# Where column weights are split, which engine squares the filters, and who ends the final norm, in a bidirectional encoder layer

## The chip, the cores and the metric

The kernel runs on one core of one Trainium2 chip, in one launch. The metric is the device time of that launch in microseconds (us); a median of several executions is compared with a median.

Five engines work side by side and wait for one another by semaphores: TensorE (PE in the rows; PEld is its loading of weights), VectorE (DVE), ScalarE (ACT), GpSimd (POOL), and SyncE (SP), whose queue issues all the DMAs spoken of here. TensorE's results land in PSUM; everything else on the chip lies in SBUF.

## The reference

One encoder layer on an input of 1024 positions by 1024 features, in float32:

```python
x = x + 0.5 * swiglu(rmsnorm(x), ffn1)      # D_FF = 2816
x = x + mixer(rmsnorm(x))
x = x + 0.5 * swiglu(rmsnorm(x), ffn2)
out = rmsnorm(x) * final_norm

# the mixer: one projection u = h @ w_in, whose columns go to three places
uc = centred_conv3(u[:, :1536])              # Hyena: x1, x2, v
k  = filters(positions)                      # small MLP, decay, scaled by rsqrt(sum k^2 + 1e-6)
z  = x1 * long_conv(v, k[0]);  z = x2 * long_conv(z, k[1])
y  = rwkv7(token_shift(u[:, 1536:3488]))     # two scans, forward and backward
g  = sigmoid(u[:, 3488:])                    # gates of the two branches
```

The filters are as long as the sequence on both sides, so the long convolutions are done as Fourier transforms.

## The kernel before

**Precision.** A float32 product of two matrices is made of three products of rounded halves: an operand x is split into hi (x rounded to the fast float32 format of TensorE) and lo (x - hi). `mm3` (L43 to L45) adds hi by hi, hi by lo and lo by hi. Activations are split once (`hThi`, `hTlo`); weights are split as they arrive: a DMA loads a block of 1024 rows by 128 columns as `w_st`, ScalarE casts it to `w_hi`, and VectorE or GpSimd subtracts to get `w_lo` (`split_from`, L30 to L37; `col_weights`, whose `lo_eng` picks the engine and is GpSimd unless said). There are two buffers of `w_st`, and three each of `w_hi` and `w_lo`.

**Stages.** ffn1 runs until about 770 us; the short convolution and the filters until 1020; the RWKV columns beside the long convolutions until about 1340; the RWKV scans and the gates until about 2070; ffn2 until 2790; its last group of down products with the final norm until the end. The order of instructions on each engine is set by the scheduler of the tile framework, which places them as their inputs come due; each engine then runs its own row in order.

**Short convolution and filters.** `mixer_in` makes twelve columns of `w_in` with `col_weights`. For each, `ShortConv` copies the product to `sh_u`/`sh_o` on ScalarE, adds two taps on VectorE (L550) and transposes on TensorE (`hy_tp`, L555). Between the columns it steps the generator `hyena_filters`, which makes four filters (two orders by two halves of 256 channels). A filter has eight steps `taps(r)`: a product `ps_h` (L420), a decay `ex` on ScalarE (L422), `kt` on VectorE (L424), its square `sq` on ScalarE (L432), and the square added to `acc` (L433); then `even_odd` (L438, L440) and products with the Fourier matrix (L448). After the last step the halves of `acc` are added (`ac2`, L499), and products with ones (L501, L506) give the sums by which the filter is scaled.

**RWKV columns beside the long convolutions.** `rwkv_columns` makes eighteen columns of `w_in`, each in two halves of 512 positions with 24 products of 128x512. `stage(j)` issues the load of column j's weights, `split(j)` makes its `w_hi` and `w_lo` on ScalarE and VectorE. Both are called in the middle of the column before:

```python
for k in range(KD):                       # KD = 8
    mm3(nc, ps, (w[0][:, k], w[1][:, k]), (hl[t][0][:, k], hl[t][1][:, k]), ...)
    if k == 3:
        if t == 0:
            split(j + 1)
            stage(j + 2)
        yield
```

At each `yield` the long convolution takes a step: forward products `hy_y<-hy_zz,F` (L627), ten or more VectorE operations `cxt` (L573, L618) that combine them and multiply by the filter's spectrum, inverse products `hy_y<-cxt,Dm` (L658), and the gate (L751, L755). A column's result goes through `rwkv_tile` (L1278: token shift on VectorE; L823 to L844: norm of the keys).

**The end.** In the last group of ffn2 eight columns d of `xT` are finished for each half t of the positions: nine products `pdn`, an add on VectorE (L226), then `nf.add`, which squares on ScalarE (`nm_sq`) and adds up on VectorE (`nm_acc`). `finish(t)` takes the reciprocal root `rms_r`, transposes `xT` back on TensorE into four PSUM buffers (L1782), multiplies each 128x512 block by `rms_r` and by the broadcast row `f_g` in one VectorE operation (L1785), and stores it (256 KB).

## Time and profile before

| | |
|---|---|
| median of 3 runs | 2841.01 us (2840.96 to 2841.77) |
| the profiled execution | 2847.4 us, of which 2845.6 us are the profiled span |
| TensorE busy | 2715.7 us, 95% of the span |
| VectorE busy | 1215.3 us, 43% |
| ScalarE busy | 893.4 us, 31% |
| GpSimd busy | 546.7 us, 19% |
| mean granted clock of TensorE | 0.973 of full speed |

The shares are means over stages that differ. Each row of a timeline gives the start, the length, the engine, the line of the kernel, the operation, the tile written and the tiles read, and in brackets how long the engine had been idle and what ended that.

### The profile page before, as it was taken

The numbers are of one execution on the slowest core, as the hardware profiler recorded it, in microseconds if no ns is written. First come the engines' busy times: TensorE is split into PE (matmuls) and PEld (weight loads), VectorE is DVE, ScalarE is ACT, GpSimd is POOL, SyncE is SP. The second block draws the span as 40 slices with busy tenths as digits, with TensorE's granted clock in tenths as the row PEclk, the third lists the DMA queues.
The fourth block names the chain that finished last, engine by engine and source line by source line (L and its number), as shares of the span: only waits on it lengthen the run. The fifth ranks groups of instructions, "written<-read, shape, count | busy, mean of one in ns | idle before, by whom it ended". The sixth has DMA issues, their size and how long they took to land. (4 is left out here: it accounts for less than half of the span.)

```text
span 2845.6 us, 45944 instructions
## 1 busy us (share of the span) xinstructions
PE 2715.7 (95%) x19440; PEld 2189.7 (77%) x19440; DVE 1215.3 (43%) x2132; ACT 893.4 (31%) x1507; POOL 546.7 (19%) x351
## 2 busy tenths in 40 slices
PE   8999999999988999999999998899999999999998
PEld 6888888888766777776787877776778888888787
DVE  4111010111547769897765767758631110101114
ACT  5111111111444542334554545532331111111113
POOL 2323232232422210000000000000033232332322
PEclk9999999999999999999999999898999999999999
DMA  5111111111341354554544325457521111111102
GB/s 127 56 41 53 44 52 45 49 48 44 112 150 63 105 169 149 173 154 129 173 133 134 104 87 183 144 178 249 151 77 56 48 48 41 56 41 49 49 26 93
DMA packets 402125, 276.43 MB, mean 97 GB/s; under 512 B 50643, under 2 KB 362527, under 8 KB 401280
## 3 DMA queue, kind: packets, MB, share of 16 engines
q1 hardware_dynamic: 401920, 273.50, 31.6%
q8 instruction: 153, 2.51, 0.4%
q14 instruction: 52, 0.43, 0.0%
HBM read 202.53 MB, written 70.91 MB: 96 GB/s over the span
## 5 line engine op out<-in xcount | busy, mean ns | idle before, releaser
L45 PE MATMUL pw<-hThi,w_lo 128*128 128x512 f32 (+1 forms) x1184 | 470.4, 398 | 15.5 <-DVE w_lo L1243 15.5
L43 PE MATMUL pw<-hThi,w_hi 128*128 128x512 f32 (+1 forms) x1184 | 472.2, 399 | 8.1 <-ACT sh_o L1265 4.5
L44 PE MATMUL pw<-hTlo,w_hi 128*128 128x512 f32 (+1 forms) x1184 | 470.8, 398 | 0.0
L33 ACT CAST w_hi<-w_st 128x1024 fp32r<-128x1024 f32 (+1 forms) x168 | 169.5, 1010 | 481.3 <-PE pw L44 185.2
L37 POOL TENSOR_TENSOR w_lo<-w_st,w_hi 128x1024 fp32r<-128x1024 f32 x100 | 239.9, 2399 | 401.0 <-ACT w_hi L33 394.7
L43 PE MATMUL pgu<-hThi,w_hi 128*128 128x512 f32 x704 | 279.1, 397 | 0.8 <-issue 0.8
L44 PE MATMUL pgu<-hTlo,w_hi 128*128 128x512 f32 x704 | 279.1, 396 | 0.3 <-POOL hTlo L37 0.2
L45 PE MATMUL pgu<-hThi,w_lo 128*128 128x512 f32 x704 | 278.9, 396 | 0.0
L43 PE MATMUL pdn<-g_hi,wd_hi 128*128 128x512 f32 x704 | 274.9, 390 | 1.8 <-DVE xT L226 1.7
L44 PE MATMUL pdn<-g_lo,wd_hi 128*128 128x512 f32 x704 | 274.6, 390 | 2.0 <-POOL g_lo L37 2.0
L45 PE MATMUL pdn<-g_hi,wd_lo 128*128 128x512 f32 x704 | 274.8, 390 | 1.7 <-POOL wd_lo L37 1.7
L45 PEld LDWEIGHTS pw<-hThi,w_lo 128*128 128x128 f32 (+1 forms) x1184 | 222.3, 188 | 69.3 <-DVE w_lo L1243 17.7
L43 PEld LDWEIGHTS pw<-hThi,w_hi 128*128 128x128 f32 (+1 forms) x1184 | 222.3, 188 | 63.0 <-ACT sh_o L1265 6.3
L226 DVE SCALAR_TENSOR_TENSOR xT<-pdn,xT 128x512 f32<-128x512 f32 x192 | 132.3, 690 | 314.8 <-PE pdn L45 314.8
L44 PEld LDWEIGHTS pw<-hTlo,w_hi 128*128 128x128 f32 (+1 forms) x1184 | 222.3, 188 | 54.2 <-issue 4.2
L209 DVE TENSOR_TENSOR silu<-silu,pgu 128x512 f32<-128x512 f32 x44 | 30.2, 687 | 449.5 <-PE pgu L45 449.5
L209 DVE TENSOR_TENSOR silu<-silu,pw 128x512 f32<-128x512 f32 x44 | 30.3, 688 | 445.8 <-PE pw L45 445.1
L37 POOL TENSOR_TENSOR wd_lo<-wdst,wd_hi 128x512 fp32r<-128x512 f32 (+1 forms) x112 | 132.1, 1180 | 333.3 <-ACT wd_hi L33 333.3
L37 POOL TENSOR_TENSOR g_lo<-silu,g_hi 128x512 fp32r<-128x512 f32 x88 | 113.5, 1289 | 399.0 <-ACT g_hi L33 399.0
L33 ACT CAST wd_hi<-wdst 128x512 fp32r<-128x512 f32 (+1 forms) x112 | 64.4, 576 | 379.2 <-PE pdn L44 365.7
L37 POOL TENSOR_TENSOR hTlo<-nm_h,hThi 128x512 fp32r<-128x512 f32 x16 | 23.6, 1477 | 737.2 <-ACT hThi L33 737.2
L43 PEld LDWEIGHTS pgu<-hThi,w_hi 128*128 128x128 f32 x704 | 132.4, 188 | 33.1 <-issue 1.2
(316 smaller groups left out, 4423.8 us busy)
## 6 DMA issues: line engine op xcount, KB each, us to landing
w_st<-in_ffn_w_gu SPq DMA_DIRECT2D x88, 512.0 KB, 3.7
w_st<-in_w_in SPq DMA_DIRECT2D x57, 512.0 KB, 3.8
wdst<-in_ffn_w_down SPq DMA_DIRECT2D x64, 256.0 KB, 2.8
wdst<-in_ffn_w_down SPq DMA_DIRECT2D x48, 192.0 KB, 2.5
d_kf<-kout SPq DMA_DIRECT2D x32, 256.0 KB, 2.3
hy_k<-d_kf SPq DMA_DIRECT2D x32, 256.0 KB, 3.1
w_st<-in_w_out SPq DMA_DIRECT2D x16, 512.0 KB, 4.4
d_X<-sh_x SPq DMA_DIRECT2D x12, 512.0 KB, 3.5
```

The source lines that it names most:

```text
L33: nc.scalar.copy(hi, src)
L37: eng.tensor_tensor(lo, src, hi.bitcast(F32), ALU.subtract)
L43: te.matmul(out, lhs[0], rhs[0], start=first, stop=False)
L44: te.matmul(out, lhs[0], rhs[1], start=False, stop=False)
L45: te.matmul(out, lhs[1], rhs[0], start=False, stop=last)
L209: nc.vector.tensor_tensor(sl, sl, pu, ALU.mult)
L226: nc.vector.scalar_tensor_tensor(xa, ps, 0.5, xa, ALU.mult, ALU.add)
```

## The change

Four places are edited.

- In the filters, the add of the squares (L433) goes from GpSimd to VectorE, and a `yield` is put between `ac2` and the product that uses it.
- In the short convolution, the twelve `w_lo` are subtracted on VectorE.
- In `rwkv_columns`, two columns are staged and split before the loop, and the loop splits column j + 2 and stages column j + 4, after the twelfth product of the first half. The 24 products of a half are put in another order: first the sixteen with `w_hi`, then the eight with `w_lo`. The numbers of buffers stay.
- In the final norm, `done` now scales `xT` in place by the weights of the norm on ScalarE, behind `nf.add`; the broadcast row `f_g` and its load go. `finish` multiplies by `rms_r` alone, the first block of each pair on VectorE, the second on ScalarE, into one tile of 128x1024, which is stored by one DMA of 512 KB.

```diff
@@ hyena_filters, taps
-                    nc.gpsimd.tensor_tensor(acc, acc, sq, ALU.add)
+                    nc.vector.tensor_tensor(acc, acc, sq, ALU.add)
@@ hyena_filters
             nc.vector.tensor_tensor(ac2, acc[:, 0], acc[:, 1], ALU.add)
+            yield
             ps = psh.tile([P, 512], F32, name="ps_h", tag="ps_h")
@@ rwkv_columns
-            stage(0)
-            stage(1)
-            split(0)
+            for j in range(2):
+                stage(j)
+            for j in range(2):
+                split(j)
+                stage(j + 2)
...
-                    for k in range(KD):
-                        mm3(nc, ps, (w[0][:, k], w[1][:, k]), (hl[t][0][:, k], hl[t][1][:, k]), k == 0, k == KD - 1, te)
-                        if k == 3:
+                    products = [(0, x, k) for k in range(KD) for x in range(2)] + [(1, 0, k) for k in range(KD)]
+                    for i, (a, b, k) in enumerate(products):
+                        te.matmul(ps, w[a][:, k], hl[t][b][:, k], start=i == 0, stop=i == 3 * KD - 1)
+                        if i == 11:
                             if t == 0:
-                                split(j + 1)
-                                stage(j + 2)
+                                split(j + 2)
+                                stage(j + 4)
                             yield
@@ mixer_in
-            weights = lambda t: col_weights(nc, wp, I["w_in"][:, ts(t, P)], KD)
+            weights = lambda t: col_weights(nc, wp, I["w_in"][:, ts(t, P)], KD, lo_eng="dve")
@@ the end
-            grow = c3.enter_context(tc.tile_pool(name="fg", bufs=1)).tile([P, D], F32, name="f_g")
-            nc.sync.dma_start(grow, bcast_row(I["final_norm"]))
+            fo = c3.enter_context(tc.tile_pool(name="fo", bufs=2))
+            def done(d, t):
+                x = xT[:, d, ts(t, 512)]
+                nf.add(x, t)
+                nc.scalar.activation(x, x, AF.Copy, scale=nf.g[:, d : d + 1])
...
+                    o = fo.tile([P, D], F32, name="f_o") if q % 2 else wp.tile([P, D], F32, name="f_w", tag="w_st")
                     for j in range(KD // 4):
...
-                        nc.vector.scalar_tensor_tensor(o, ps.rearrange("p a b -> p (a b)"), r[:, q : q + 1],
-                                                       grow[:, ts(j, 512)], ALU.mult, ALU.mult)
-                        nc.sync.dma_start(out[0, ts(ORDER[i], P), ts(j, 512)], o)
+                        flat = ps.rearrange("p a b -> p (a b)")
+                        if j:
+                            nc.scalar.activation(o[:, ts(j, 512)], flat, AF.Copy, scale=r[:, q : q + 1])
+                        else:
+                            nc.vector.tensor_scalar(o[:, ts(j, 512)], flat, r[:, q : q + 1], None, ALU.mult)
+                    nc.sync.dma_start(out[0, ts(ORDER[i], P), :], o)
```

Three places show how the scheduler's rows of instructions move. The first is VectorE's row in the first long convolution, just before its first inverse products; `cxt` are the convolution's operands, and the numbers behind the names count tiles. Before, this `w_lo` stands there:

```order
L573 TENSOR_TENSOR cxt_7327<-cxt_7263,cxt_7285 128x1024
L573 TENSOR_TENSOR cxt_7328<-cxt_7263,cxt_7285 128x1024
L1243 TENSOR_TENSOR w_lo_7351<-w_st_7258,w_hi_7350 128x1024
L573 TENSOR_TENSOR cxt_7370<-cxt_7325 128x512 x2
L573 TENSOR_TENSOR cxt_7373<-cxt_7327 128x512 x2
L573 TENSOR_TENSOR cxt_7376<-cxt_7370,cxt_7373 128x512 x2
```

And in the changed kernel:

```order
L574 TENSOR_TENSOR cxt_7335<-cxt_7271,cxt_7293 128x1024
L574 TENSOR_TENSOR cxt_7336<-cxt_7271,cxt_7293 128x1024
L1244 TENSOR_TENSOR w_lo_7359<-w_st_7167,w_hi_7358 128x1024
L574 TENSOR_TENSOR cxt_7378<-cxt_7333 128x512 x2
L574 TENSOR_TENSOR cxt_7381<-cxt_7335 128x512 x2
L574 TENSOR_TENSOR cxt_7384<-cxt_7378,cxt_7381 128x512 x2
```

VectorE's row is the same at this place; the `w_lo` in it is another. TensorE's row at the same place, around the first inverse products, is before:

```order
L45 MATMUL pw_7379<-hThi1_119,w_lo_7255 128x512
L43 MATMUL pw_7448<-hThi0_111,w_hi_7350 128x512
L44 MATMUL pw_7448<-hTlo0_112,w_hi_7350 128x512
L43 MATMUL pw_7594<-hThi1_119,w_hi_7350 128x512
L44 MATMUL pw_7594<-hTlo1_120,w_hi_7350 128x512
L43 MATMUL pw_7648<-hThi0_111,w_hi_7461 128x512
L44 MATMUL pw_7648<-hTlo0_112,w_hi_7461 128x512
L45 MATMUL pw_7448<-hThi0_111,w_lo_7351 128x512
```

And in the changed kernel, where `w_lo_7359` of VectorE's row is read only behind the inverse products:

```order
L1262 MATMUL pw_7602<-hThi1_119,w_lo_7263 128x512 x8
L1262 MATMUL pw_7656<-hThi0_111,w_hi_7358 128x512
L1262 MATMUL pw_7656<-hTlo0_112,w_hi_7358 128x512
...
L1262 MATMUL pw_7656<-hThi0_111,w_hi_7358 128x512
L659 MATMUL hy_y_7400<-cxt_7384,Dm_6967 128x256 x4
L659 MATMUL hy_y_7438<-cxt_7405,Dm_6967 128x256 x4
```

Before, TensorE reads the `w_lo` of VectorE's row six products after the last column ended; after, it comes to the inverse products first and reads that `w_lo` behind them. The third place is ScalarE's row at the end, for columns 4 and 5 of the last group; `nm_sq_23266` is column 4's square and `wd_hi_23272` is column 5's weight (in the row of before, `nm_sq_23264` and `wd_hi_23269`). Before:

```order
L33 CAST wd_hi_23249<-wdst_23247 128x384
L33 CAST wd_hi_23269<-wdst_23267 128x384
L92 ACTIVATE nm_sq_23224<-xT_18189 128x512
L92 ACTIVATE nm_sq_23244<-xT_18189 128x512
L33 CAST wd_hi_23289<-wdst_23287 128x384
L92 ACTIVATE nm_sq_23264<-xT_18189 128x512
```

And in the changed kernel:

```order
L1783 ACTIVATE xT_18189<-xT_18189,k_final_norm_76 128x512
L92 ACTIVATE nm_sq_23266<-xT_18189 128x512
L33 CAST wd_hi_23272<-wdst_23270 128x384
L1783 ACTIVATE xT_18189<-xT_18189,k_final_norm_76 128x512
L33 CAST wd_hi_23293<-wdst_23291 128x384
L33 CAST wd_hi_23314<-wdst_23312 128x384
```

Column 5's cast moved from ahead of column 2's square to behind column 4's, and a scale `xT` (L1783) follows each square.

## Rows read from the trace of the kernel before

**Rows 1.** Page: busy time, share of the span and instructions of each engine.

```profile
PE 2715.7 (95%) x19440; PEld 2189.7 (77%) x19440; DVE 1215.3 (43%) x2132; ACT 893.4 (31%) x1507; POOL 546.7 (19%) x351
```

**Rows 2.** Stretches: length, busy of PE PEld DVE ACT POOL, TensorE clock, DMA share, GB/s.

```profile
770.00:1020.00 250.00, 229.35 (x938) 166.99 (x937) 163.48 (x318) 120.27 (x191) 66.87 (x42) 0.97 0.30 99
2790.00:2846.00 56.00, 46.62 (x233) 38.26 (x231) 34.15 (x59) 19.62 (x34) 15.44 (x15) 0.92 0.35 118
1060.00:1332.00 272.00, 251.13 (x1150) 201.00 (x1149) 252.72 (x373) 94.97 (x136) 0.00 (x0) 0.97 0.50 151
1100.00:1110.00 10.00, 6.39 (x16) 4.62 (x16) 10.00 (x15) 1.04 (x1) 0.00 (x0) 0.66 0.37 112
```

**Rows 3.** Waits of TensorE, 1020 to 1400 us: total us, times, longest.

```profile
PE pw L45 <- DVE w_lo L1243: 15.5, 5, 6.5
```

**Rows 4.** Timeline near 1100 us, TensorE, then VectorE: start, length, [idle before].

```profile
1103.57 0.80 PE L45 MATMUL pw<-hThi,w_lo 128*128 128x512 f32 x1 [3.48 <-DVE w_lo L1243]
1097.02 5.36 DVE L573 TENSOR_TENSOR cxt<-cxt 128x512 f32<-128x512 f32 x7
```

**Rows 5.** Waits of VectorE, 1062 to 1332 us.

```profile
DVE hr_v L823 <- PE psA L820: 7.8, 3, 5.0
```

**Rows 6.** Timeline near 1175 us, TensorE, then VectorE.

```profile
1178.99 0.50 PE L45 MATMUL pw<-hThi,w_lo 128*128 128x512 f32 x1 [2.26 <-DVE w_lo L1243]
1173.01 0.17 DVE L823 TENSOR_SCALAR hr_v<-psA 128x16 f32<-128x16 f32 x1 [4.95 <-PE psA L820]
```

**Rows 7.** Groups by form, 770 to 1020 us: busy, mean ns of one, idle before.

```profile
L550 DVE SCALAR_TENSOR_TENSOR sh_o<-sh_u,k_cw,sh_o 128x1024 f32<-128x1024 f32 x20 | 31.6, 1582 | 21.7 <-ACT sh_o L545 21.6
L433 POOL TENSOR_TENSOR acc<-acc,sq 128x512 f32<-128x512 f32 x28 | 38.3, 1366 | 89.3 <-ACT sq L432 78.6 <-PE ps_k L448 10.7
L37 POOL TENSOR_TENSOR w_lo<-w_st,w_hi 128x1024 fp32r<-128x1024 f32 x9 | 21.9, 2433 | 73.5 <-ACT w_hi L33 67.4 <-PE ps_k L448 6.1
```

**Rows 8.** The same, 1020 to 1350 us, where GpSimd is idle.

```profile
L1243 DVE TENSOR_TENSOR w_lo<-w_st,w_hi 128x1024 fp32r<-128x1024 f32 x16 | 19.5, 1216 | 3.9 <-ACT w_hi L1242 3.9
L550 DVE SCALAR_TENSOR_TENSOR sh_o<-sh_u,k_cw,sh_o 128x1024 f32<-128x1024 f32 x4 | 5.1, 1278 | 0.0
```

**Rows 9.** Timeline in the first filter, VectorE, then GpSimd.

```profile
852.00 0.69 DVE L424 TENSOR_TENSOR kt<-ps_h,ex 128x512 f32<-128x512 f32 x1 [0.49 <-ACT ex L422]
871.95 1.26 POOL L433 TENSOR_TENSOR acc<-acc,sq 128x512 f32<-128x512 f32 x1 [3.94 <-ACT sq L432]
```

**Rows 10.** Waits of TensorE, 740 to 1020 us.

```profile
PE ps_h L501 <- DVE ac L499: 6.9, 4, 4.3
```

**Rows 11.** Timeline of VectorE, first two columns of the short convolution.

```profile
801.19 3.67 DVE L550 SCALAR_TENSOR_TENSOR sh_o<-sh_u,k_cw,sh_o 128x1024 f32<-128x1024 f32 x2 [10.62 <-ACT sh_o L545]
808.73 4.58 DVE L550 SCALAR_TENSOR_TENSOR sh_o<-sh_u,k_cw,sh_o 128x1024 f32<-128x1024 f32 x2 [3.74 <-ACT sh_o L545]
```

**Rows 12.** Timeline of the end: ScalarE, GpSimd, TensorE, VectorE.

```profile
2822.33 0.51 ACT L33 CAST wd_hi<-wdst 128x384 fp32r<-128x384 f32 x1 [1.61 <-DMA wdst<-in_ffn_w_down]
2826.88 0.63 ACT L92 ACTIVATE nm_sq<-xT 128x512 f32<-128x512 f32 x1 [0.46 <-DVE xT L226]
2826.50 1.02 POOL L37 TENSOR_TENSOR wd_lo<-wdst,wd_hi 128x384 fp32r<-128x384 f32 x1 [2.58 <-ACT wd_hi L33]
2823.77 0.47 PE L43 MATMUL pdn<-g_hi,wd_hi 128*128 128x512 f32 x1 [1.11 <-DVE xT L226]
2825.89 0.39 PE L43 MATMUL pdn<-g_hi,wd_hi 128*128 128x512 f32 x1
2837.82 3.65 PE L1782 MATMUL f_ps<-ident,xT 128*128 128x128 f32 x16 [2.33 <-issue]
2839.85 2.80 DVE L1785 SCALAR_TENSOR_TENSOR f_o<-f_ps,rms_r,f_g 128x512 f32<-128x512 f32 x4 [0.16 <-PE f_ps L1782]
```

**Rows 13.** DMA issues: queue, count, KB each, us to landing.

```profile
out<-f_o SPq DMA_DIRECT2D x16, 256.0 KB, 2.3
d_X<-sh_x SPq DMA_DIRECT2D x12, 512.0 KB, 3.5
```

More of the change, by code (lines that the diff above doesn't have):

```diff
@@ L1782, in finish @@
                             nc.tensor.transpose(ps[:, c, :], xT[:, 4 * j + c, ts(i, P)], ident)
-                        o = np_.tile([P, 512], F32, name="f_o", tag="nm_h") if j else \
-                            wp.tile([P, 512], F32, name="f_o", tag="w_st")
-                        nc.vector.scalar_tensor_tensor(o, ps.rearrange("p a b -> p (a b)"), r[:, q : q + 1],
-                                                       grow[:, ts(j, 512)], ALU.mult, ALU.mult)
-                        nc.sync.dma_start(out[0, ts(ORDER[i], P), ts(j, 512)], o)
+                        flat = ps.rearrange("p a b -> p (a b)")
[4 more added lines that the diff above has]
+                    nc.sync.dma_start(out[0, ts(ORDER[i], P), :], o)
             def pools():
@@ L1793, in hybrid_layer_kernel @@
             for _ in ffn(nc, pools, wp, xT, live["hl"], I["ffn2_w_gu"], I["ffn2_w_down"],
-                         lambda d, t: nf.add(xT[:, d, ts(t, 512)], t), finish):
+                         done, finish):
                 pass
```

## The prediction

> **What bounds the kernel now.** The page comes first: TensorE is busy 95% of the span [rows 1], so a change that adds no product and removes none can only win back pauses, and all pauses together are 130 us. The order of instructions differs in two stretches (the mixer's front, about 770 to 1380 us, and the last group of ffn2), so the rest is priced at nothing: the same rows on every engine, except the short stretch of ffn1's end, where three subtractions move to a VectorE that waits. The windows then show two different stretches. In the convolutions and columns, 1060 to 1332 us, TensorE is busy 251.1 of 272 us and VectorE 252.7: they wait for each other. In the short convolution, 770 to 1020, VectorE has 86 us idle, and TensorE loses 21. In the last 56 us TensorE loses 9 [rows 2].
>
> The waits of TensorE name the cause in the columns: five waits of 15.5 us in all for a `w_lo`, the longest 6.5 [rows 3]. The timeline shows what such a wait is. The `w_lo` is a subtraction of 1.22 us, but seven operations of the long convolution, 5.36 us from 1097.02 on, stand ahead of it on VectorE, and TensorE stands 3.48 us until it is done [rows 4, 8]. The clock follows: in the ten microseconds behind this wait the granted clock is 0.66, a mean between full speed (2.4 GHz) and half, and TensorE's busy time is 6.39 of 10 [rows 2]. So the reader should see a late operand on an engine that is itself full, not an engine that was asked too late.
>
> **The columns.** Splitting two columns ahead leaves VectorE's work as it is: eighteen subtractions, sixteen of them in this stretch at 1216 ns [rows 8]; two now stand ahead of the loop. What moves is who waits for which operation. In the order of the changed kernel the `w_lo` that stands in the first convolution's chain is read behind the inverse products, so the five waits of 15.5 us should go. But VectorE's operations before those inverse products are the same, and TensorE, which no longer stands at the `w_lo`, comes to them earlier and waits there for `cxt`. What can be won is therefore VectorE's idle time, since TensorE can only run ahead as far as VectorE does: 272 - 252.7 = 19.3 us [rows 2], the upper end. Not all of it comes from late `w_lo`. VectorE waits 7.8 us in three places for `psA`, the norm of the keys [rows 5]; the longest, 4.95 us, ends at 1173.01, and TensorE then stands 2.26 us for the `w_lo` that VectorE could not yet do [rows 6]. There each engine waits in turn for the other, and a weight two columns ahead cuts the circle. The rest of the idle time is waits for a Fourier product or an inverse product just issued, which the change leaves. I take the 4.95 us, as **5 us**. The lower end is 0: every wait for `w_lo` becomes one for `cxt`. A loss needs more VectorE work ahead of a chain, at most the two early subtractions, 2.4 us.
>
> With four stagings ahead and still two buffers of `w_st`, the load for column j + 4 waits until column j + 2 is split, and the next cast on ScalarE waits for that load; what is queued behind such a cast is the copy of a finished column out of PSUM, for which TensorE waits in turn. With the split two columns early the load has a whole column more to land; I put this at 0, and it lies within the 5.
>
> **The short convolution and the filters.** Twelve subtractions go from GpSimd (2433 ns each) to VectorE (1216 ns), and 28 adds of the squares from GpSimd (1366 ns) to VectorE [rows 7, 8]. No VectorE add of this form has a row in this place; a 128x512 operation with two inputs takes 0.69 us [rows 9], so VectorE gets 12 x 1.22 + 28 x 0.69 = 34 us more. Three effects reach TensorE.
> First, GpSimd's own work slows VectorE: the two taps (L550) take 1582 ns in the mean here and 1278 ns where GpSimd is idle [rows 7, 8]. The first two pairs, for which TensorE's transposes wait, take 3.67 and 4.58 us [rows 11]; undisturbed they are 2 x 1.28 = 2.56. In the changed order the first subtraction stands ahead of the first pair, inside VectorE's idle 10.62 us, and the second within the second pair, where it adds 1.22. That saves 3.67 - 2.56 = 1.1 and 4.58 - 2.56 - 1.22 = 0.8, together **1.9 us**. The upper end is the excess of all 20, 20 x 0.304 = 6.1.
> Second, at the end of each of the four filters TensorE stands for the sum of squares, 6.9 us in all, 4.3 of it in the first [rows 10]. The last add takes 1.26 us on GpSimd [rows 9] and 0.69 on VectorE: 0.57 sooner, four times, **2.3 us**. The ends are 0 and 6.9.
> Third, the cost. In the first filter no dense product lies beside the taps. VectorE waits there 0.49 us a tap for the decay factor [rows 9]; an add of 0.69 fills this and puts 0.20 more on each of seven taps, **1.4 us**. In the other three filters the 21 adds lie beside columns of the projection, under VectorE's idle 86 us, and I price them at nothing; if that cover were gone they would cost 21 x 0.69 = 14.5 us. The extra `yield` only puts other products ahead of the sum's, and costs nothing.
> Sum here: 1.9 + 2.3 - 1.4 = 2.8 us won, between 13 won (6.1 + 6.9) and 15.9 lost (1.4 + 14.5).
>
> **The end.** The two final operations of each pair now run on two engines. Now the last eight take until 2839.85 + 2.80 = 2842.65, while the transposes, 16 in 3.65 us behind 2837.82, end at 2841.47 [rows 12]. They run at 0.228 us each, and cannot start before a PSUM buffer is free, so the changed kernel ends its last block at 2841.47 + 0.68 = 2842.15: **0.5 us** won, not half of the VectorE time. Then the last store is 512 KB and not 256: stores of 256 KB land in 2.3 us, and the nearest transfer of 512 KB, also a write, in 3.5 [rows 13]: **1.2 us** lost. The Trainium skill (DMA: Bandwidth & Descriptors, Rules for kernel authors) speaks for the larger store: it asks for transfers of 1 MiB or more. By the fit that the skill gives (SBUF — State Buffer, The DMA setup-cost knee; 2 us and the bytes by 436 GB/s) 256 KB more cost an estimated 0.6 us, and the sum would be 0.6 us smaller. No row shows a large store at the end of the span, when nothing hides it.
> The half before wins: TensorE's wait of 1.11 us for VectorE between the transposes of the first half [rows 12] should go, since four of its eight operations are ScalarE's: **1.1 us** won.
> The new scales stand on ScalarE, and with them the casts of the down weights move. Column 5's cast ran at 2822.33, four columns of products ahead of its use; in the changed order it stands behind column 4's square, which starts at 2826.88 and takes 0.63 [rows 12]. So it ends at 2826.88 + 0.63 + 0.51 = 2828.02, and column 5's products, which start at 2825.89, nine products or 2.12 us behind column 4's first, start 2.1 us later. The low half follows on GpSimd, 1.02 us, while two products of 0.24 run: 0.5 more. Four transposes, at full clock half of the 0.228, fill 0.4 of it. So **2.2 us** lost; columns 6 and 7 have their casts in time, and the scales themselves lie under products. The ends are 0 (the scheduler's row waits less than I think) and, if TensorE's clock falls to 1.2 GHz behind this pause for the 27 products left, 2.2 + 27 x 0.24 = 8.7.
> Sum here: -0.5 + 1.2 - 1.1 + 2.2 = 1.8 us lost.
>
> **Sum.** -5.0 - 2.8 + 1.8 = -6.0 us. Against the profiled execution's 2847.4 us this is 2841.4; that execution lies 6.4 us above the median of the runs, so on the median 2841.0 - 6.0 = **2835.0 us**. A measurement of this kernel tells a change from none beyond about 0.2%, 5.7 us, so the forecast lies on this line, with 2835.3 its border.
>
> **Rivals.**
> *VectorE's idle time is all won.* The waits for `w_lo` go, none for `cxt` comes, and the clock stays up. For it: 15.5 us of waits with one name. Against it: VectorE is busy 93% of the stretch, and 10.00 of 10 us around the wait at 1103 [rows 2]. 19.3 + 2.8 - 1.8 = 20.3 us won, 2820.7 us.
> *The wait only changes its name.* VectorE sets the pace throughout, and what was waited at `w_lo` is waited at the inverse products. For it: VectorE's row is the same at the place shown in the order. Against it: the 4.95 us in which VectorE itself waits. 0 - 2.8 + 1.8 = 1.0 won, 2840.0 us, within 0.2%.
> *The filters' adds are exposed.* `kt`, the even and odd parts and the spectrum's sums form a chain through VectorE; an add put between them delays the next `kt` in the later filters too. 14.5 - 6.0 = 8.5 us lost, 2849.5 us. It is slower beyond 0.2% once 17 of the 21 adds are on the path (11.7 / 0.69). For it: the change's order puts each add ahead of the next `kt`. Against it: 86 us idle, and columns beside it.
>
> **How the numbers follow.** The forecast gets 0.45, its own range 2828 to 2841, three fifths of it below 2835.3; the first rival 0.13, the second 0.26 (nearly all within 0.2%), the third 0.16. So faster: 0.13 + 0.27 + 0.03 = 0.43; slower 0.17; within 0.2% the remaining 0.40. The range cuts about half of the outer rivals away on each side: 2822 to 2848.
>
> **What would show it.** Right: no wait for `w_lo` in the columns, new waits of the inverse products for `cxt`, VectorE's idle time from 1060 to 1332 about 5 us less; `psA` waited for less. L550 near 1280 ns; the wait for the sum of squares near 4.6 us; no idle time of VectorE ahead of `kt` in the first filter. At the end, a pause of about 2 us ahead of column 5's products, a last store of over 3 us. Wrong: TensorE's waits in the columns below 5 us in all (first rival) or above 20 (second); waits for `kt` or `eo` in filters 2 to 4 (third); a lower granted clock in a stretch where this text has no pause.

## The result and the profile after

The changed kernel takes 2824.69 us (median of 6 runs, 2821.21 to 2833.47); the kernel before takes 2842.59 beside it (6 runs, 2840.96 to 2846.41). The ratio is 0.9942, its 95% interval 0.9927 to 0.9956: 0.58% faster, some 16.5 us (12.5 to 20.8). The direction and the range held; the forecast was 10.3 us too high.

The profiled execution of the changed kernel took 2829.45 us, with a span of 2827.7 and a mean granted clock of 0.977: 17.9 us of span less than before. Its page has this row of busy times, which answers to [rows 1]:

```profile
PE 2707.4 (96%) x19440; PEld 2185.7 (77%) x19440; DVE 1229.4 (43%) x2164; ACT 909.0 (32%) x1531; POOL 480.3 (17%) x311
```

TensorE's busy time fell by 8.3 us at the same 19440 products (fewer of them ran at the slower clock), so about half of the gain is a pause less and half a product that ran faster. To see where the time went, the same product is looked up in both timelines of TensorE, and the differences of the starts are taken:

| start of | before | after | difference | products of TensorE ahead of it, before and after | gained in the stage, for the same products |
|---|---|---|---|---|---|
| the first transpose of the short convolution, `hy_tp` | 805.1 | 803.0 | -2.1 | 3445, 3445 | 2.1 |
| the last `ps_k` of the filters | 1021.1 | 1010.6 | -10.5 | 4258, 4271 | 11.3 |
| the last inverse product of the long convolutions | 1330.4 | 1317.2 | -13.2 | 5569, 5595 | 5.7 |
| the first product of the scans, `psA<-rl_x,rw_w` | 1343.3 | 1324.8 | -18.5 | 5612, 5612 | -0.6 |
| the last product of the gates, `mo_ps` | 2083.2 | 2062.5 | -20.7 | 16175, 16175 | 2.2 |
| the first transpose of the final norm, `f_ps` | 2808.1 | 2788.7 | -19.4 | 19288, 19288 | -1.3 |
| the last transpose | 2841.0 | 2823.1 | -17.9 | 19439, 19439 | -1.4 |

Two of these places don't stand at the same amount of work. TensorE's row was put in another order, so that 13 more of the 128x512 products of the projection stand ahead of the last `ps_k`, and 26 more ahead of the last inverse product; at the scans the count is equal again. Such products start 0.227 us apart at full clock, so these are 3.0 and 5.9 us, and the last column counts them in; this is an estimate. The starts alone would give 8.4, 2.7 and 5.3 us for the filters, the columns and the handover to the scans, and the last two of these would mislead. The busy times agree with the column. Here are the stretches from the first transpose to the last `ps_k` and from there to the scans (columns as in [rows 2]), before, then in the changed kernel:

```profile
805.00:1021.00 216.00, 200.10 (x813) 144.28 (x814) 144.49 (x281) 108.99 (x171) 57.72 (x36) 0.97 0.29 91
1021.00:1343.00 322.00, 297.16 (x1356) 237.91 (x1354) 278.13 (x418) 111.84 (x162) 0.96 (x1) 0.98 0.52 162
```

```profile
803.00:1011.00 208.00, 200.08 (x828) 147.20 (x829) 161.19 (x318) 111.11 (x173) 0.00 (x0) 0.98 0.31 97
1011.00:1325.00 314.00, 294.34 (x1342) 236.07 (x1343) 275.52 (x417) 110.83 (x159) 0.96 (x1) 0.98 0.54 167
```

TensorE's idle time fell from 15.9 to 7.9 us in the first and from 24.8 to 19.7 in the second.

What a single trace can tell is seen in kernels that share an order of instructions. With the final norm's edit alone, a kernel is the one before up to ffn2, and its starts in the table lie 0.3 to 1.1 us from those of before as far as the scans, and 3.8 at their last state product; with the columns' edit alone the filters are those of before, and end 2.3 us later. The seven traces that have the whole filters' edit and no dead work lie within 3.6 us of one another at the last `ps_k`. So up to 1340 us a difference of two or three us between two starts is not safe by itself, and the 2.2 us of the scans and gates are no gain of the change.

**The filters.** The waits of TensorE from 740 to 1020 us, of the changed kernel (total us, times, longest):

```profile
PE ps_h L502 <- DVE ac L499: 3.4, 1, 3.4
PE ps_h L420 <- DVE kt L424: 2.3, 3, 0.8
...
PE hy_tp L556 <- DVE sh_o L551: 0.7, 1, 0.7
```

And three of VectorE's groups by form, 760 to 1010 us:

```profile
L551 DVE SCALAR_TENSOR_TENSOR sh_o<-sh_u,k_cw,sh_o 128x1024 f32<-128x1024 f32 x20 | 25.6, 1279 | 8.1 <-ACT sh_o L546 8.0
L433 DVE TENSOR_TENSOR acc<-acc,sq 128x512 f32<-128x512 f32 x28 | 19.3, 689 | 3.7 <-ACT sq L432 3.7
L525 DVE TENSOR_TENSOR kout<-cxt 128x256 f32<-128x256 f32 x18 | 7.6, 422 | 1.9 <-DMA d_kf<-kout 1.8
```

The taps take 1279 ns, as forecast (1582 in [rows 7]); the sums wait once and not four times [rows 10]; VectorE does its 28 adds and the twelve subtractions without TensorE's waiting for it elsewhere. The windows show the rest (columns as in [rows 2]; the first answers to its first row):

```profile
770.00:1020.00 250.00, 238.30 (x990) 177.33 (x989) 185.01 (x365) 125.50 (x196) 6.54 (x5) 0.97 0.32 103
1050.00:1318.00 268.00, 250.95 (x1152) 201.29 (x1151) 251.84 (x378) 93.86 (x135) 0.96 (x1) 0.98 0.51 156
```

TensorE is busy 238.3 of 250 us and not 229.4, with 52 more products done in the window; VectorE's idle time fell from 86 us to 65.

**The columns.** The waits of TensorE from 1010 to 1400 us no longer hold a `w_lo` above 1 us (before: [rows 3]):

```profile
PE pw L1262 <- ACT sh_o L1270: 7.4, 2, 5.6
PE hy_y L659 <- DVE cxt L619: 2.4, 1, 2.4
PE pw L1262 <- ACT sh_o L1274: 2.2, 1, 2.2
```

And `psA` is waited for less (VectorE's waits, 1050 to 1320 us; before: [rows 5]):

```profile
DVE hr_v L824 <- PE psA L821: 4.4, 3, 2.7
```

So 15.5 us of waits with one name went; those whose releaser is ScalarE's copy of a finished column, 4.5 us before (longest 3.2), are 9.6; and of TensorE's idle time from the filters' end to the scans 5.2 us were won. The longest wait now is followed in the timelines of TensorE, ScalarE and VectorE, in this order:

```profile
1152.87 0.79 PE L1262 MATMUL pw<-hThi,w_hi 128*128 128x512 f32 x1 [5.58 <-ACT sh_o L1270]
```

```profile
1151.18 1.04 ACT L1317 COPY sh_v<-rw_kh 128x1024 f32<-128x1024 f32 x1 [3.26 <-issue]
1152.13 1.26 ACT L1270 ACTIVATE sh_o<-pw,k_mu 128x512 f32<-128x512 f32 x2
```

```profile
1149.70 1.40 DVE L1297 SCALAR_TENSOR_TENSOR rw_kh<-sh_o,k_kk,psA 128x512 f32<-128x512 f32 x2
```

TensorE needs the PSUM buffer that ScalarE empties at 1152.13. ScalarE stands 3.26 us ahead of that, because the reversed copy `sh_v` is next in its row and reads `rw_kh`, which VectorE starts at 1149.70, in line behind the convolution's `cxt`, and ends at 1151.10. In this place the column waits for VectorE as before, by way of another engine.

**The handover to the scans.** Here are SP's queue and TensorE before, then both in the changed kernel:

```profile
1339.09 0.42 SPq L899 DMA_DIRECT2D rl_x<-d_tw  x1
1343.29 1.16 PE L55 MATMUL psA<-rl_x,rw_w 64*128 64x128 f32 x16 [3.15 <-DMA rl_x<-d_tw]
```

```profile
1311.20 0.88 SPq L900 DMA_DIRECT2D rl_x<-d_tw  x1
1318.47 0.63 PE L762 MATMUL hy_t<-ident,hy_z 128*128 128x128 f32 x4 [0.87 <-DVE hy_z L756]
1320.26 0.50 PE L55 MATMUL pw<-hThi,w_hi 128*128 128x512 f32 x1 [1.16 <-ACT hy_zT L764]
1324.80 1.16 PE L55 MATMUL psA<-rl_x,rw_w 64*128 64x128 f32 x16
```

Before, `rl_x` was loaded behind the last inverse product, and TensorE stood 3.15 us for it. In the changed kernel the RWKV columns end first, the load goes 6 us ahead of that product, and this wait is gone. But nothing is won here: the 26 products of these columns that ran between the last inverse product and the scans now run earlier, TensorE waits 0.87 and 1.16 us in their place, and the granted clock from 1317 to 1325 us is 0.78, where it was 1.00 from the last inverse product to the scans before.

**The start of ffn2.** The -1.3 us of the table is no scatter. The stage takes 724.3 to 725.0 us in the twelve traces without the norm's edit and 726.2 and 726.3 in the two with it. The broadcast row `f_g` was loaded at its start; without that load the first two down weights are issued together, and GpSimd has two `wd_lo` in one go beside the reciprocal root of ffn2's norm. GpSimd and VectorE before, then GpSimd, VectorE and TensorE in the changed kernel:

```profile
2090.02 1.27 POOL L37 TENSOR_TENSOR wd_lo<-wdst,wd_hi 128x512 fp32r<-128x512 f32 x1 [3.15 <-ACT wd_hi L33]
2089.60 0.17 DVE L71 TENSOR_SCALAR rms_e<-rms_e 128x4 f32<-128x4 f32 x1
```

```profile
2068.85 2.50 POOL L37 TENSOR_TENSOR wd_lo<-wdst,wd_hi 128x512 fp32r<-128x512 f32 x2 [2.68 <-ACT wd_hi L33]
2068.90 1.25 DVE L71 TENSOR_SCALAR rms_e<-rms_e 128x4 f32<-128x4 f32 x1
2070.18 1.18 DVE L72 TENSOR_TENSOR rms_r<-rms_r,rms_e 128x4 f32<-128x4 f32 x1
2071.83 1.19 PE L114 MATMUL nm_ps<-nm_d,ones_c 128*128 128x128 f32 x4 [1.24 <-DVE nm_d L113]
```

Two operations of 128x4, of 0.17 and 0.16 us before, take 1.25 and 1.18 and end with GpSimd's; in the traces without the norm's edit at most one of the two is held. TensorE comes to the product that needs them 9.4 us behind the last product of the gates in both traces with the edit, and 7.5 to 8.4 us behind it in the other twelve.

**The end.** TensorE's timeline shows the pause ahead of column 5 (the first two rows), and the last transposes at the slower clock (0.55 granted, as 0.50 before):

```profile
2806.71 0.50 PE L43 MATMUL pdn<-g_hi,wd_hi 128*128 128x512 f32 x1 [1.35 <-ACT wd_hi L33]
2807.91 0.50 PE L45 MATMUL pdn<-g_hi,wd_lo 128*128 128x512 f32 x1 [0.46 <-POOL wd_lo L37]
...
2819.89 3.48 PE L1793 MATMUL f_ps<-ident,xT 128*128 128x128 f32 x16 [1.99 <-ACT f_w L1796]
```

On ScalarE the cast stands behind column 4's square, as the order had it:

```profile
2805.62 0.63 ACT L92 ACTIVATE nm_sq<-xT 128x512 f32<-128x512 f32 x1 [0.65 <-DVE xT L226]
2806.16 0.49 ACT L33 CAST wd_hi<-wdst 128x384 fp32r<-128x384 f32 x1
```

And the stores from the buffer of the last one (KB each, us to landing) answer to [rows 13]:

```profile
out<-f_o SPq DMA_DIRECT2D x4, 512.0 KB, 3.3
```

### The profile page after: what moved, and what is told of

Read it like the earlier page. It is cut to its first block, busy times and chain, and to the rows that moved or that the text cites. A ratio compares the mean times of both kernels' runs of the same rounds, so it can differ in the third digit from the quotient of the medians.

```text
span 2827.7 us, 45877 instructions
## 1 busy us (share of the span) xinstructions
PE 2707.4 (96%) x19440; PEld 2185.7 (77%) x19440; DVE 1229.4 (43%) x2164; ACT 909.0 (32%) x1531; POOL 480.3 (17%) x311
## 3 DMA queue, kind: packets, MB, share of 16 engines
q1 hardware_dynamic: 400624, 272.97, 31.7%
## 5 line engine op out<-in xcount | busy, mean ns | idle before, releaser
L43 PE MATMUL pw<-hThi,w_hi 128*128 128x512 f32 x896 | 358.2, 400 | 3.5 <-ACT sh_o L546 3.4
L44 PE MATMUL pw<-hTlo,w_hi 128*128 128x512 f32 x896 | 356.3, 398 | 0.0
L45 PE MATMUL pw<-hThi,w_lo 128*128 128x512 f32 x896 | 355.5, 397 | 0.0
L33 ACT CAST w_hi<-w_st 128x1024 fp32r<-128x1024 f32 (+1 forms) x168 | 169.4, 1010 | 474.2 <-PE pw L44 184.4
L37 POOL TENSOR_TENSOR w_lo<-w_st,w_hi 128x1024 fp32r<-128x1024 f32 x88 | 210.8, 2396 | 316.9 <-ACT w_hi L33 316.8
L43 PEld LDWEIGHTS pw<-hThi,w_hi 128*128 128x128 f32 x896 | 169.3, 189 | 44.1 <-ACT sh_o L546 4.4
L44 PEld LDWEIGHTS pw<-hTlo,w_hi 128*128 128x128 f32 x896 | 169.2, 189 | 41.3 <-issue 4.6
L45 PEld LDWEIGHTS pw<-hThi,w_lo 128*128 128x128 f32 x896 | 169.2, 189 | 39.2 <-issue 2.1
L45 PEld LDWEIGHTS pgu<-hThi,w_lo 128*128 128x128 f32 x704 | 132.7, 188 | 31.9
```

The costliest lines, as they stand in the source:

```text
L33: nc.scalar.copy(hi, src)
L37: eng.tensor_tensor(lo, src, hi.bitcast(F32), ALU.subtract)
L43: te.matmul(out, lhs[0], rhs[0], start=first, stop=False)
L44: te.matmul(out, lhs[0], rhs[1], start=False, stop=False)
L45: te.matmul(out, lhs[1], rhs[0], start=False, stop=last)
```

## The experiments

The filters' edit here is the adds of the squares, the extra `yield` and the twelve `w_lo` on VectorE; the other two are the columns' and the norm's. Two theories stood against each other. By the first, the gain up to 1340 us is GpSimd's absence: its work held VectorE and so the filters' chain, and the columns' edit only keeps what the filters win. By its rival, the split two columns ahead is the gain, as the 15.5 us of waits suggest. The later runs ask which part of the filters' edit, and of the columns', does the work. Each ratio is to the kernel before on the same chip; the traces compared are of several chips. Since the order of TensorE's products differs, the traces are read over one stretch in which all these kernels do the same 2167 products, from the first `hy_tp` to the first product of the scans:

| kernel | us | of which TensorE idle | mean granted clock |
|---|---|---|---|
| before | 538.2 | 41.0 | 0.975 |
| the norm's edit alone | 537.4 | 40.0 | 0.975 |
| the columns' edit alone | 535.1 | 34.0 | 0.968 |
| the filters' edit alone | 534.8 | 33.6 | 0.958 |
| the whole change | 521.8 | 27.6 | 0.977 |
| all but the norm's edit, first and second time | 521.4, 520.3 | 26.3, 25.3 | 0.974, 0.974 |
| the same, with the weights back on GpSimd | 530.3 | 32.8 | 0.971 |
| the same, with the adds back on GpSimd | 524.7 | 29.5 | 0.974 |
| the same, with dead adds on GpSimd | 529.6 | 31.7 | 0.971 |
| the same, only split two ahead | 525.4 | 29.0 | 0.974 |
| the same, only the new order | 521.4 | 27.6 | 0.977 |

Kernels that agree in this stretch lie within 1.5 us.

**The columns' edit alone.** The kernel before with that part of the diff.

> The kernel before with the edit of rwkv_columns alone (two columns staged and split ahead, products with w_hi first). By the prediction, 5 us faster. By what the trace of the changed kernel seems to show, 8 us faster: 2 to 3 from the last filter to the last inverse product, because VectorE sets the pace there, and some 5 between that product and the first product of the scans. By the rival that all of VectorE's idle time is won, 15 or more, all of it ahead of the last inverse product. By the rival that the wait only changes its name, within 2 us of before.

2841.01 us, ratio 0.9994 (0.9979 to 1.0009): between 6.0 us won and 2.6 lost, so the median can't tell the forecast's 5 us from no change. The waits for `w_lo` go, and the wait for ScalarE's copy is there as in the full change (TensorE, 1000 to 1345 us):

```profile
PE pw L1260 <- ACT sh_o L1268: 5.6, 1, 5.6
```

In the trace TensorE idles 7.0 us less over the stretch of the table. The scans start 3.6 us sooner than before, though the filters, which are those of before with the same products ahead of their end, end 2.3 us later: from there to the scans 5.9 us are won. The rival, 15 us or more, falls.

**The filters' edit alone.**

> The kernel before with the squares' adds and the twelve w_lo of the short convolution on VectorE, and the extra yield. By the prediction, 2.8 us faster. By the trace of the changed kernel, 10 us faster: 2 at the end of ffn1 and about 2 in each of the four filters, so the gain lies wherever GpSimd worked beside VectorE. By the rival that the adds are exposed, 8 us slower.

2832.48 us, ratio 0.9959 (0.9945 to 0.9974). In the trace the filters end 12.4 us sooner, with 13 more products done, but the scans start only 7.5 us sooner. From the filters' end to the scans the waits are much the ones of before: those for `w_lo` stay, and VectorE waits for `psA` longer (TensorE's row, then VectorE's, 1000 to 1345 us; compare [rows 3, 5]). What fell there is the clock, to 0.95 from 0.98 before (the third row):

```profile
PE pw L45 <- DVE w_lo L1244: 14.8, 4, 6.2
```

```profile
DVE hr_v L824 <- PE psA L821: 11.2, 3, 8.2
```

```profile
1009.00:1336.00 327.00, 301.24 (x1343) 241.69 (x1343) 277.25 (x418) 110.18 (x159) 1.00 (x1) 0.95 0.51 158
```

This trace is of the longest of the kernel's seven executions, 10.2 us above their median, so it may show too small a gain.

**The norm's edit alone.**

> The kernel before with the edit of the final norm alone. By the prediction and by the trace of the changed kernel, 1.5 to 2 us slower: a pause ahead of column 5's products and a later landing of the last store. By the rival that ScalarE's half of the last step is what counts, 2 us faster.

2846.09 us, ratio 1.0019 (1.0004 to 1.0033): a loss of 1 to 9 us, and in the trace, from the last product of the gates to the last transpose, 760.3 us where before took 757.9 and the traces without this edit 757.1 to 758.4. This edit costs, some 2.5 us by the traces.

**All but the norm's edit.**

> The changed kernel with the final norm of before. If the parts add up, 1.5 to 2 us faster than the changed kernel, and 18 to 20 us faster than before; if the norm's edit helps, slower than the changed kernel by what it brought.

2822.01 us, ratio 0.9926 (0.9908 to 0.9944); run again as the last experiment, 2824.44, 0.9945 (0.9925 to 0.9964):

> The kernel e4 once more, as the reference of the three above on the same chip, and to see whether its time repeats: 0.993 of before by e4's first run.

The filters end 12.0 and 13.1 us sooner, the scans start 19.8 and 21.4 us sooner. The filters' edit had 7.5 of this by itself and the columns' 3.6. In the table the idle time adds up: 7.4 and 7.0 us less with one edit, 14.7 and 15.7 with both. So neither theory holds alone: each edit takes its own waits away. What doesn't add is the speed of the products between the pauses, by the clock. Against the full change (0.9942) no difference can be told; the norm's loss is below what medians of six runs resolve.

**The weights back on GpSimd.** From here on each kernel is the last one, all but the norm's edit, with one thing changed.

```diff
-            weights = lambda t: col_weights(nc, wp, I["w_in"][:, ts(t, P)], KD, lo_eng="dve")
+            weights = lambda t: col_weights(nc, wp, I["w_in"][:, ts(t, P)], KD)
```

> The kernel without the norm's edit (e4), with the twelve w_lo of the short convolution back on GpSimd; the squares' adds stay on VectorE. By the theory that GpSimd's work slows VectorE's work beside it: VectorE's taps are slow again near the twelve subtractions (mean above 1400 ns), the end of ffn1 and the first transposes lose their 3 us, and 5 us of e4's gain go. By the prediction's terms, 1.9 us go.

2836.79 us, ratio 0.9964 (0.9948 to 0.9981). The filters end at 1020.8, where they ended before (1021.1), though with 15 more products done. Over the stretch of the table this kernel takes 4.8 us less than the columns' edit alone (2 or 3 of them may be that trace's late filters), so the adds on VectorE win a little by themselves; and 8.9 and 10.0 us more than with the subtractions on VectorE too. The waits at the transposes are back (TensorE, 730 to 1040 us):

```profile
PE ps_h L420 <- DVE kt L424: 4.2, 5, 1.6
...
PE ps_h L502 <- DVE ac L499: 3.4, 1, 3.4
PE hy_tp L556 <- DVE sh_u L540: 1.9, 1, 1.9
PE hy_tp L556 <- DVE sh_o L551: 1.5, 2, 1.3
```

Only the sums' wait stays short, so that one belongs to the adds.

**The adds back on GpSimd.**

```diff
-                    nc.vector.tensor_tensor(acc, acc, sq, ALU.add)
+                    nc.gpsimd.tensor_tensor(acc, acc, sq, ALU.add)
```

> The kernel without the norm's edit (e4), with the squares' adds back on GpSimd; the subtractions stay on VectorE. By the theory that GpSimd's work slows VectorE's: filters 2 to 4 lose about 2 us each, 6 to 8 us of e4's gain go. By the prediction's terms (the last add 0.57 sooner, four times, less 1.4 in the first filter), 1 us goes. If VectorE's new adds had cost the path something, this kernel would be faster than e4.

2829.0 us, ratio 0.9931 (0.9910 to 0.9953), not to be told from the kernel with them on VectorE. The filters end at 1011.7, 2.6 us later, and the sums' waits are back: 6.3 us in four places against 3.4 in one. Over the stretch of the table the adds are worth 3.3 and 4.4 us by the two traces without this step, the subtractions 8.9 and 10.0.

**GpSimd's work added again, as dead work.** A result that nobody reads is added on GpSimd in each of the 28 taps, and a second subtraction for each of the twelve columns.

```diff
+                    nc.gpsimd.tensor_tensor(spare, sq, sq, ALU.add)
...
+        nc.gpsimd.tensor_tensor(x, st, hi.bitcast(F32), ALU.subtract)
```

> The kernel without the norm's edit (e4), with work on GpSimd that nothing waits for: in each of the 28 taps a sum of the square with itself into a spare tile, and with each of the twelve weights of the short convolution a second subtraction into a spare tile. VectorE does all that it does in e4. By the theory that GpSimd slows VectorE by reading SBUF beside it, VectorE's taps take 1500 ns or more again, and 4 to 8 us of e4's gain go. By the theory that only GpSimd's own late results were waited for, the time is e4's within 2 us.

2856.27 us, ratio 1.0036 (1.0021 to 1.0050). This one doesn't tell what it was made for: the dead subtraction also holds `w_st`, and TensorE stood 23.0 us in one place for a `w_hi`, which no other kernel shows. So the dead adds were tried by themselves (the first line of the diff alone):

> e4 with one more sum on GpSimd in each of the 28 taps, of the square with itself into a spare tile that nothing reads; no second subtractions. By the theory that GpSimd's reading beside VectorE slows VectorE, the even and odd parts eo rise from 420 to 450 ns or more, and 2 to 4 us of the time to the last filter are lost. If e6's small loss came from the late sum of squares alone, this kernel keeps e4's time to the last filter within 1 us.

2829.64 us, ratio 0.9951 (0.9933 to 0.9968); the medians leave it open whether this is slower than without them, but in the trace the filters end at 1018.0, 9 to 10 us later, with nothing added to any other engine. Three of VectorE's groups there, 770 to 1020 us:

```profile
L433 DVE TENSOR_TENSOR acc<-acc,sq 128x512 f32<-128x512 f32 x28 | 20.9, 747 | 3.7 <-ACT sq L432 3.7
L440 DVE TENSOR_TENSOR eo<-kt 128x256 f32<-128x256 f32 x32 | 15.2, 475 | 0.7
...
L527 DVE TENSOR_TENSOR kout<-cxt 128x256 f32<-128x256 f32 x18 | 9.7, 540 | 1.0 <-DMA d_kf<-kout 0.9
```

689, 421 and 422 ns in the changed kernel are 747, 475 and 540 here, and the sums wait 5.7 us in four places again. The timeline shows what such a mean hides, GpSimd first, then VectorE:

```profile
850.98 1.50 POOL L435 TENSOR_TENSOR spare<-sq 128x512 f32<-128x512 f32 x1 [60.54 <-ACT sq L432]
852.98 1.04 POOL L435 TENSOR_TENSOR spare<-sq 128x512 f32<-128x512 f32 x1 [0.51 <-ACT sq L432]
```

```profile
850.89 0.68 DVE L433 TENSOR_TENSOR acc<-acc,sq 128x512 f32<-128x512 f32 x1
853.01 1.55 DVE L433 TENSOR_TENSOR acc<-acc,sq 128x512 f32<-128x512 f32 x1
```

The VectorE add that starts first takes its 0.68, and GpSimd's takes 1.50; where GpSimd's starts 0.03 us first, it takes 1.04 and VectorE's takes 1.55, until 0.54 behind GpSimd's end. No other engine has more to do in this kernel, so GpSimd's work by itself made the filters late, through VectorE. The Trainium skill (SBUF — State Buffer, SBUF: two separate sides) says that the two engines share a pair of ports, that a VectorE operation with two SBUF inputs contends with a GpSimd operation that reads SBUF, and that whoever starts first has the pair for its whole instruction. These rows agree with it to about 0.15 us: behind the other's end VectorE takes 0.54 us and GpSimd 0.91, where the whole operations take 0.68 and 1.04.

**Only the split two ahead** (the old order of the products) and **only the new order** (split one ahead):

> e4 with the products of a column in the old order; the columns are still split two ahead. By the theory that the earlier split does the work, no wait for a w_lo is left that could use the cover of sixteen products, and the time is e4's within 3 us. By the rival that the order of the products does it, 5 us slower than e4.

2826.36 us, 0.9944 (0.9931 to 0.9956).

> e4 with the columns split one ahead as before; the products with w_hi still come first. Sixteen products cover some 3.6 us of each late w_lo, so of the waits of 3.5, 2.3, 6.5, 1.6 and 1.7 us only some 3 us stay. By the theory that the earlier split does the work (it also lets the last column end ahead of the last inverse products, so that the scans' loads go out early), 5 us or more slower than e4. By the rival, e4's time within 3 us.

2824.55 us, 0.9934 (0.9917 to 0.9952). By the medians either half gives what both give. Over the stretch of the table the new order gives it too (521.4 us), with TensorE still waiting for `w_lo`, but for 6.4 us in three places and not 15.5 in five. The split alone takes 4.0 and 5.1 us more than both, though its waits for `w_lo` are 1.5 us in one place; one trace each is little for such a difference, and the cause was not looked for.

**The reversed copies on GpSimd.** This was to take the wait of 5.58 us away, by taking `sh_v` out of ScalarE's row.

```diff
-            nc.scalar.copy(x, o[:, ::-1])
+            nc.gpsimd.tensor_copy(x, o[:, ::-1])
```

> The kernel without the norm's edit (e4), with the reversed copies sh_v in the RWKV columns on GpSimd instead of ScalarE. In e4 TensorE stands 5.6 us for a PSUM tile that ScalarE has not copied out, since a reversed copy stands ahead of it and waits for VectorE's result. If that order on ScalarE is the cause, this wait goes, and up to 5 us are won; if GpSimd's copies slow VectorE, which sets the pace there, by 1 us each, sixteen of them take this back and more: up to 10 us slower than e4.

2858.64 us, ratio 1.0042 (1.0024 to 1.0059). The copy takes 4.64 us on GpSimd and 1.05 on ScalarE, and ScalarE's next write of `sh_o` waits for it, 17.0 us in three places; TensorE's waits for `sh_o` grew to 10.8 us. It moved the wait and didn't remove it, so it doesn't price ScalarE's queue.

## Why the prediction was right, and where it was too small

**What bounds it** held: no product was added or removed, and only pauses and the clock behind them were won.

**The short convolution and the filters: -2.8 forecast, -8.4 measured by the starts and -11.3 for the same products.** This term was mis-sized most. Its mechanism is shown: GpSimd's work held VectorE. But it was priced by two pairs of taps, 1.9 us. TensorE's waits add up to more. At the transposes behind the first they were 4.6 us before (2.7 and 1.9 by their releasers) and are 0.7. At the sums 6.9 and 3.4: in filters 2 to 4 the wait went whole, 2.6 us, where the working took 0.57 a filter. For `eo` 1.6 and 0.6. For `kt` 1.4 and 2.3, which is the first filter's cost: 1.0 us of it lies there, forecast 1.4. Together 3.9 + 3.5 + 1.0 - 0.9 = 7.5, close to the 8.0 by which TensorE's idle time fell; the other 3 us are products that ran faster. From 880 to 930 us the granted clock was 0.92 before and is 0.99. The step that failed is reading 1582 ns as an even slowdown of every tap. Before, the median of the 20 is 1281 ns and the longest 3265: seven of them are held, and the rest run as if alone. The longest is the second tap of the second pair in [rows 11], from 810.05 to 813.32 us, beside this `w_lo`:

```profile
809.71 2.52 POOL L37 TENSOR_TENSOR w_lo<-w_st,w_hi 128x1024 fp32r<-128x1024 f32 x1 [7.25 <-ACT w_hi L33]
```

TensorE's transpose behind it waited the 1.9 us. The second pair's subtraction, counted as 1.22 us against the change, cost nothing: the scheduler had put the transposes behind five more products. Which edit it is: both parts, the twelve subtractions for the larger share (9 to 10 us of the stretch when they are put back, the adds 3 to 4).

**ffn1's end: 0 forecast, -2.1 measured.** By itself this is near what a trace tells; but of the nine traces with the twelve subtractions on VectorE and no dead ones on GpSimd, eight are 2.1 to 4.7 us ahead here (the ninth, with the dead adds, 1.2), and the three that have them on GpSimd 0.3 to 0.7. GpSimd and TensorE before:

```profile
729.02 2.41 POOL L37 TENSOR_TENSOR w_lo<-w_st,w_hi 128x1024 fp32r<-128x1024 f32 x1 [3.03 <-ACT w_hi L33]
731.38 1.30 POOL L37 TENSOR_TENSOR g_lo<-silu,g_hi 128x512 fp32r<-128x512 f32 x1
732.63 1.98 POOL L37 TENSOR_TENSOR wd_lo<-wdst,wd_hi 128x384 fp32r<-128x384 f32 x2
733.69 0.50 PE L45 MATMUL pdn<-g_hi,wd_lo 128*128 128x512 f32 x1 [1.09 <-POOL wd_lo L37]
```

What was looked at was the VectorE that takes the subtractions, and not the GpSimd that gives them up: there a `w_lo` stood ahead of a `wd_lo` that TensorE needed. These waits went from 1.7 us to 0.3.

**The columns: -5 forecast, -5.1 measured from the filters' end to the scans for the same products.** The size held, and the longest wait for `psA` fell from 5.0 us to 2.7, as the term had it; with the columns' edit alone it is 5.9 us. The waits for `w_lo` were not simply lost, though: a part of them took another name. That name was less `cxt` (2.4 and 0.9 us) than ScalarE's copy. The working had seen that a finished column's copy out of PSUM is queued on ScalarE, and priced that at 0 for another operand, the load of `w_st`; the copy stood behind `sh_v`. VectorE's idle time fell by 3.1 us (19.3 of 272 before, 16.2 of 268 after, beside 1150 and 1152 products), not 5, so the bound by which the term was made held. The loads at the handover, of which the working says nothing, go out 28 us sooner, but by the count of products the handover changed by no more than 1.0 us either way in any trace with this edit.

**Edits together.** The prediction added its terms. In TensorE's waits that is right: over the stretch of the table 7.4 and 7.0 us went with one edit, 13.4 to 15.7 with both. In time it is not decided: 3.4 and 3.1 us alone, 16.4 to 17.9 together. But with one edit the products ran at a lower clock, and with the columns' edit alone it was lower in the filters (0.953 from the first transpose to the last `ps_k`, 0.968 before), which that edit leaves as they were; so there it is scatter, and the trace of the filters' edit alone is of the longest of seven executions. The medians don't resolve it (0.41% and 0.06% against 0.74% and 0.55%).

**The rivals.** The first rival's time, 2820.7, is nearer than the forecast, but not its mechanism: VectorE's idle time was not all won. The second, a wait that only changes its name, fell with the 5.1 us of the columns. The third, exposed adds, fell too: with the adds off VectorE again the stretch was no shorter, but 3 to 4 us longer.

**The norm's edit: +1.8 forecast, all at the end; +1.4 measured there and +1.3 at the start of ffn2.** The stage of ffn2 was priced at nothing, for the same rows on every engine; but `f_g`'s load was one of its rows, and without it GpSimd's work fell beside VectorE's, the mechanism of the filters once more. At the end, the pause ahead of column 5 is 1.8 us idle (1.35 and 0.46), forecast 2.2, and the first half's wait of 1.11 us is gone; the waits for the sum of squares grew from 0.6 to 1.5 us, which no term had. Behind the last transpose nothing changed, 4.6 us to the end of the span in both: the last store is issued 0.6 us sooner (0.5 forecast), and lands later by as much, 3.55 us from its issue to the end of the span where 2.94 were taken before. The prediction's sum had 1.2 for this, and 0.6 as the other figure. That no half-clock followed the pause also held: the rows behind it are at 0.23 us a product. By the medians of that edit alone it costs 1 to 9 us, which holds both the 1.8 and the 2.7.

**Left open.** Of the scans and gates' 2.2 us nothing is claimed. That stage is 732 to 743 us long in the fourteen traces, with the same number of products in it; why it varies was not tried. What sets the clock between the filters and the scans, and what ScalarE's queue costs the columns, was not settled either.

## What to carry to other kernels

Taking work off an engine is to be priced on both sides: not only whether the receiver has room, but which operations stand behind the moved one on the giver, and which of the receiver's own it had held. Where two engines hold each other, read the longest and the median of a group, since a mean of 1582 ns was 1281 for most and up to 3265 for those that TensorE waited for. Where a change puts an engine's row in another order, count the products ahead of each place before two starts are compared: 26 products moved ahead of a landmark looked like 5 us won behind it. And a load that is taken out moves those behind it, and with them the work of other engines.

## What the runs showed of the hardware

- GpSimd adds whose results nobody reads made the filters end 9 to 10 us later: 28 adds of 1.38 us in the mean, with VectorE's `kout` at 540 ns in the mean and not 422, while their median stayed at 418 and the longest was 1259. Single operations are held, not all slowed.
- A VectorE operation of 128x4 took 1.25 us beside GpSimd's subtractions (two in 2.50 us), and 0.17 where GpSimd was idle.
- A reversed copy of 128x1024 takes 4.64 us on GpSimd and 1.05 on ScalarE.
- With the same order of instructions, starts agree within 3.6 us at the end of the filters, and the stage of the scans and gates differs by up to 11; so stretches compared ahead of the scans resolve what medians of six runs (some 0.15% either way, 4 us) can't.
